# Letting each store wait for its own tile's product alone, in a streaming SwiGLU kernel

## Chip, cores and metric

The kernel runs on one core of a Trainium2 chip. The metric is device time in microseconds (us). The profile's span runs from the first to the last instruction of one profiled execution and is 1.8 us shorter than the time of that same execution. A ratio is the mean time of one kernel's fast runs over that of the other's fast runs of the same rounds, so it is not quite the ratio of the medians that are quoted beside it.

## The reference

```python
def setup_inputs():
    return {"x": np.random.randn(8192, 8192).astype(np.float32)}

def reference(x):
    a, b = np.split(x, 2, axis=-1)
    silu_b = b / (1 + np.exp(-b))
    return a * silu_b
```

It reads 268 MB, writes 134 MB, and does one activation and one product for each output element.

## The kernel before

The rows are cut into 32 tiles of 128 partitions with two rows each. Three slots in SBUF, the on-chip memory, take turns. Every load and store is split over the core's 16 DMA engines, each of which moves its share piece by piece (one partition's bytes are one piece, 64 KB for a whole load). SyncE's transfers go through the queue q1, ScalarE's through q10. SyncE issues the loads; ScalarE applies silu in place and issues the stores of tiles 0 to 29; VectorE multiplies. One semaphore, `prod`, counts all products, and a store waits until it has reached the count known at the moment when the store is written down:

```python
    def store(i, eng, c0=0, cw=R * half):
        s = i % BUFS
        eng.wait_ge(prod_sem, counts["prod"])
        inst = eng.dma_start(
            out=ov[i * P : (i + 1) * P, c0 : c0 + cw], in_=slots[s][:, c0 : c0 + cw]
        )
        # ... (completion to store_sem, or to end_sem for the last three tiles)

        # ... (the first three loads)
        for i in range(last):                    # last = 31
            # ... (tile 0 is computed in two halves)
                swiglu(i)
            if i == last - 1:
                swiglu(last, 0, 1)               # first half of tile 31
            store(i, nc.scalar if i < last - 1 else nc.sync)
            # ... (load of tile i + 3; tile 31 comes in two halves)
        store(last, nc.sync, 0, half)            # called 31a below
        for c0 in range(0, half, half // 2):
            swiglu(last, 1, 2, c0, half // 2)    # third and fourth quarter of tile 31
        store(last, nc.sync, half, half)         # called 31b below
        nc.sync.wait_ge(end_sem, 16 * counts["end"])
```

The first half of tile 31 is written down between tile 30's product and its store. So store 30 waits for 33 products, though 32 would do. Every other store already waits for its own tile alone.

Of the kernel before, what the change touches and what calls it, by code (L numbers as in the profile page):

```python
# [1 line left out]

# [4 lines left out]

_SILU = mybir.ActivationFunctionType.Silu


@with_exitstack
def kernel(
    ctx: ExitStack,
    tc: tile.TileContext,
    x: bass.AP,
    out: bass.AP,
):




    nc = tc.nc
    N, M = x.shape
    half = M // 2
    P = nc.NUM_PARTITIONS
    R = 2
    BUFS = 3

    xv = x.tensor.reshape([N // R, R * M]).ap()  # L30
    ov = out.tensor.reshape([N // R, R * half]).ap()
    ntiles = N // (P * R)
    last = ntiles - 1

    pool = ctx.enter_context(tc.tile_pool(name="sbuf", bufs=1))
    slots = [pool.tile([P, R * M], x.dtype, name=f"slot{s}") for s in range(BUFS)]
    load_sem = [tc.alloc_semaphore(f"load{s}") for s in range(BUFS)]
    store_sem = [tc.alloc_semaphore(f"store{s}") for s in range(BUFS)]
    last_sem = tc.alloc_semaphore("last")
    gate_sem = tc.alloc_semaphore("gate")  # L40
    prod_sem = tc.alloc_semaphore("prod")
    end_sem = tc.alloc_semaphore("end")

    def load(i, c0=0, cw=R * M):
        s = i % BUFS
        if i >= BUFS:
            nc.sync.wait_ge(store_sem[s], 16 * (i // BUFS))
        nc.sync.dma_start(  # L48
            out=slots[s][:, c0 : c0 + cw], in_=xv[i * P : (i + 1) * P, c0 : c0 + cw]
        ).then_inc(last_sem if c0 else load_sem[s], 16)  # L50

    counts = {"gate": 0, "prod": 0, "end": 0}

    def rows(ap, k0, k1, pitch, c0, cw):
        return ap[:, k0 * pitch : k1 * pitch].rearrange("p (r w) -> p r w", w=pitch)[
            :, :, c0 : c0 + cw
        ]

    def swiglu(i, k0=0, k1=R, c0=0, cw=half):
        s = i % BUFS  # L60
        xt = slots[s]
        b = rows(xt, k0, k1, M, half + c0, cw)
        if i == last and k0:
            nc.scalar.wait_ge(last_sem, 16)
        else:
            nc.scalar.wait_ge(load_sem[s], 16 * (i // BUFS + 1))
        nc.scalar.activation(out=b, in_=b, func=_SILU).then_inc(gate_sem, 1)  # L67
        counts["gate"] += 1
        if k0:
            nc.vector.wait_ge(prod_sem, counts["prod"])  # L70
        nc.vector.wait_ge(gate_sem, counts["gate"])  # L71
        nc.vector.tensor_mul(  # L72
            out=rows(xt, k0, k1, half, c0, cw), in0=rows(xt, k0, k1, M, c0, cw), in1=b
        ).then_inc(prod_sem, 1)
        counts["prod"] += 1

    def store(i, eng, c0=0, cw=R * half):
        s = i % BUFS
        eng.wait_ge(prod_sem, counts["prod"])
        inst = eng.dma_start(  # L80
            out=ov[i * P : (i + 1) * P, c0 : c0 + cw], in_=slots[s][:, c0 : c0 + cw]
        )
        if i + BUFS <= last:
            inst.then_inc(store_sem[s], 16)
        else:
            inst.then_inc(end_sem, 16)
            counts["end"] += 1

    with tc.tile_critical(no_gpsimd_drain=True):  # L89
        for i in range(BUFS):  # L90
            load(i)
        for i in range(last):
            if i == 0:
                for k in range(R):
                    swiglu(i, k, k + 1)
            else:
                swiglu(i)
            if i == last - 1:
                swiglu(last, 0, 1)
            store(i, nc.scalar if i < last - 1 else nc.sync)  # L100
            nxt = i + BUFS
            if nxt < last:
                load(nxt)
            elif nxt == last:
                load(last, 0, M)
                load(last, M, M)
        store(last, nc.sync, 0, half)
        for c0 in range(0, half, half // 2):
            swiglu(last, 1, 2, c0, half // 2)
        store(last, nc.sync, half, half)  # L110
        nc.sync.wait_ge(end_sem, 16 * counts["end"])


# [1 line left out]
_INS = ['x']  # L115
_OUTS = [((8192, 4096), 'float32')]


# [23 lines left out]
```

## Time and profile before

| what | value |
|---|---|
| time, median of the first 3 runs | 936.82 us (936.62 to 937.01) |
| span of the profiled run | 935.0 us |
| moved | 402.67 MB |
| DMA engines | busy in every slice, 434 to 435 GB/s in the middle |
| VectorE, ScalarE busy | 30%, 24% |

Such a page is read from the resource that is never idle. Here it is the 16 DMA engines. The shares of VectorE and ScalarE only say that they are not it. The lines stand in the prediction below. Three more of this profile: SyncE's own waits (total us, times, longest), the page's row of the single 4 MB store of SyncE (the last number is the us from issue to landing), and a window of 1.5 us around the moment in question (columns as in the prediction):

```profile
SPq L80 <- DVE slot L72: 37.0, 2, 29.6
...
out_dram<-slot SPq DMA_DIRECT2D x1, 4096.0 KB, 11.3
...
912.50:914.00 1.50, 0.29 (x1) 0.00 (x0) 0.00 (x0) 1.00 0.83 350
```

The longest wait, 29.6 us, is the one ahead of store 30. In the trace's transfer records, cut into half microseconds, the 1.5 us around its end (912.5 to 914.0) are the only place between 50 us and the very end where the 16 engines together are busy for less than 97%.

### The profile page before, as it was taken

What the parts mean: (1) busy time and instruction counts of PE and PEld (TensorE: products, weight loads), DVE (VectorE), ACT (ScalarE), POOL (GpSimd) and SP (SyncE); (2) the same over time, 40 slices, a digit from 0 to 9 for tenths busy, and PEclk for the clock granted to TensorE, in tenths of its full rate; (3) what the DMA queues carried; (4) which work ended last, traced back from release to release, by engine and by line L of the source; (5) the groups of instructions that cost most, each with busy time, mean ns of one, the idle gap of its engine ahead of it and who ended that gap; (6) DMA issues with size and microseconds to landing.
All of it is one profiled execution on the core that took longest, in us unless ns stands there. A gap on an engine that the chain in (4) does not pass through costs nothing.

```text
span 935.0 us, 192 instructions
## 1 busy us (share of the span) xinstructions
DVE 278.6 (30%) x35; ACT 226.6 (24%) x36; POOL 0.2 (0%) x4
## 2 busy tenths in 40 slices
DVE  0333213332133321333312333123331233321352
ACT  0233320233302333113331133311333203332041
POOL 0000000000000000000000000000000000000000
DMA  9999999999999999999999999999999999999998
GB/s 404 401 446 428 429 440 428 436 428 450 426 423 444 428 439 436 430 429 457 422 423 451 414 446 430 429 437 435 428 437 450 414 453 419 432 443 426 428 443 366
DMA packets 9505, 402.67 MB, mean 431 GB/s; under 512 B 1056, under 2 KB 1056, under 8 KB 1056
## 3 DMA queue, kind: packets, MB, share of 16 engines
q1 hardware_dynamic: 5184, 276.83, 68.6%
q10 hardware_dynamic: 4320, 125.83, 31.2%
q14 instruction: 1, 0.01, 0.0%
HBM read 268.44 MB, written 134.22 MB: 431 GB/s over the span
## 4 chain that ended last, share of the span: by engine, by line
DMA 81%; DVE 10%; ACT 8%; issue 0%; SPq 0%; DVEq 0%
DMA slot<-in_x_dram 41%; DMA out_dram<-slot 39%; DVE slot L72 10%; ACT slot L67 8%; SPq L48 0%; SPq L137 0%; DVEq L71 0%; SPq L89 0%
## 5 line engine op out<-in xcount | busy, mean ns | idle before, releaser
L72 DVE TENSOR_TENSOR slot<-slot 128x8192 f32<-128x8192 f32 (+2 forms) x35 | 278.6, 7961 | 642.4 <-ACT slot L67 642.3
L67 ACT ACTIVATE slot<-slot 128x8192 f32<-128x8192 f32 (+2 forms) x35 | 225.3, 6443 | 690.6 <-DMA slot<-in_x_dram 690.6
L67 ACT ACT_TABLE_LOAD x1 | 1.3, 1283 | 0.9 <-SPq L89 0.9
L126 POOL MEMSET const-bfloat16-1.0<- 128x1 bf16 x1 | 0.1, 101 | 0.0
L126 POOL MEMSET const-uint8-127<- 128x1 uint8 x1 | 0.1, 101 | 0.0
L126 POOL MEMSET const-float32-0.0<- 128x1 f32 x1 | 0.1, 98 | 0.2 <-issue 0.2
L126 POOL MEMSET const-float32-1.0<- 128x1 f32 x1 | 0.1, 98 | 0.0
## 6 DMA issues: line engine op xcount, KB each, us to landing
out_dram<-slot ACTq DMA_DIRECT2D x30, 4096.0 KB, 36.7
slot<-in_x_dram SPq DMA_DIRECT2D x2, 4096.0 KB, 27.0
out_dram<-slot SPq DMA_DIRECT2D x1, 4096.0 KB, 11.3
out_dram<-slot SPq DMA_DIRECT2D x2, 2048.0 KB, 14.2
slot<-in_x_dram SPq DMA_DIRECT2D x31, 34.4
```

The costliest lines, as they stand in the source:

```text
L67: nc.scalar.activation(out=b, in_=b, func=_SILU).then_inc(gate_sem, 1)
L72: nc.vector.tensor_mul(out=rows(xt, k0, k1, half, c0, cw), in0=rows(xt, k0, k1, M, c0, cw), in1=b).then_inc(prod_sem, 1)
L126: nc = _bacc.Bacc("TRN2", target_bir_lowering=False, num_devices=1)
```

## The change

Each store is to wait for its own tile's product count. Only the wait of store 30 becomes another: 32 in place of 33.

```diff
     counts = {"gate": 0, "prod": 0, "end": 0}
+    done = {}
@@ swiglu
         counts["prod"] += 1
+        done[i] = counts["prod"]
@@ store
-        eng.wait_ge(prod_sem, counts["prod"])
+        eng.wait_ge(prod_sem, done[i])
```

## The prediction

> **What bounds the kernel now.** I read the page first, then a table of windows over the steady part, then the timeline of the last 40 us, then windows well under a microsecond wide around the two moments that matter. From the page:
>
> ```profile
> span 935.0 us, 192 instructions
> DVE 278.6 (30%) x35; ACT 226.6 (24%) x36; POOL 0.2 (0%) x4
> DMA  9999999999999999999999999999999999999998
> q1 hardware_dynamic: 5184, 276.83, 68.6%
> q10 hardware_dynamic: 4320, 125.83, 31.2%
> ```
>
> VectorE and ScalarE work for less than a third of the span; the 16 DMA engines are busy in every slice. q1 is the queue of SyncE (all loads, and the last three stores), q10 that of ScalarE (30 stores). The windows (columns: stretch, width, busy time of DVE, ACT, POOL, clock, share of the DMA engines, GB/s) say how full:
>
> ```profile
> 100.00:500.00 400.00, 121.70 (x14) 98.41 (x14) 0.00 (x0) 1.00 1.00 435
> 500.00:880.00 380.00, 113.00 (x13) 91.38 (x13) 0.00 (x0) 1.00 1.00 434
> ```
>
> Share 1.00: there is no gap to close in the middle. The compute time that the chain of waits shows lies beside other tiles' transfers. Only the head, the tail, or a gap near the tail can give anything, and nothing but the tail is touched. The timeline of the tail (start, length, engine, line, operation):
>
> ```profile
> 894.85 8.69 DVE L72 TENSOR_TENSOR slot<-slot 128x8192 f32<-128x8192 f32 x1 [20.31 <-ACT slot L67]
> 904.71 3.62 ACT L67 ACTIVATE slot<-slot 128x4096 f32<-128x4096 f32 x1 [9.90 <-DMA slot<-in_x_dram]
> 908.36 4.42 DVE L72 TENSOR_TENSOR slot<-slot 128x4096 f32<-128x4096 f32 x1 [4.82 <-ACT slot L67]
> 912.81 8.59 SPq L80 DMA_DIRECT2D out_dram<-slot  x3
> 914.42 3.71 ACT L67 ACTIVATE slot<-slot 128x2048 f32<-128x2048 f32 x2 [6.09 <-DMA slot<-in_x_dram]
> 916.43 4.62 DVE L72 TENSOR_TENSOR slot<-slot 128x2048 f32<-128x2048 f32 x2 [3.65 <-ACT slot L67]
> ```
>
> Tile 30's product ends at 894.85 + 8.69 = 903.54, but its store is issued at 912.81, after the product of tile 31's first half (908.36 + 4.42 = 912.78). So the needless wait is real, 9.25 us long. But is any DMA engine short of work meanwhile? Until about 912.4 none is: load 31 still runs. Around 913 some are:
>
> ```profile
> 912.45:912.78 0.33, 0.33 (x1) 0.00 (x0) 0.00 (x0) 1.00 0.01 0
> 912.78:912.84 0.06, 0.01 (x1) 0.00 (x0) 0.00 (x0) 1.00 2.54 1092
> 912.84:913.65 0.81, 0.00 (x0) 0.00 (x0) 0.00 (x0) 1.00 0.00 0
> 913.65:913.81 0.16, 0.00 (x0) 0.00 (x0) 0.00 (x0) 1.00 6.75 2867
> 913.81:913.98 0.17, 0.00 (x0) 0.00 (x0) 0.00 (x0) 1.00 0.00 0
> 913.98:914.06 0.08, 0.00 (x0) 0.00 (x0) 0.00 (x0) 1.00 1.91 819
> ...
> 932.59:932.80 0.21, 0.00 (x0) 0.00 (x0) 0.00 (x0) 1.00 2.57 1092
> 932.80:932.86 0.06, 0.00 (x0) 0.00 (x0) 0.00 (x0) 1.00 1.28 546
> ```
>
> In such a table a transfer counts where it starts, so GB/s times width, over the piece size (32 KB for these loads and store 30, 16 KB for the half stores of tile 31), counts the pieces begun. 912.78:912.84: 1092 x 0.06 = 65.5 KB, two pieces. Nothing for 0.81 us. 913.65:913.81: 2867 x 0.16 = 459 KB, fourteen pieces. 913.98:914.06: 819 x 0.08 = 65.5 KB, two again. At the end, fourteen last pieces of 16 KB (229 KB) start by 932.80 and two last ones after it.
>
> So the engines are not alike. Fourteen finish load 31 early, stand idle, and begin store 30 at 913.65 to 913.81. **Two engines are late**: they start their last load piece at 912.78 to 912.84. A piece takes 1.213 us (the DMA view of 904 to 912.45: 99.6% of 16 engines' 8.45 us over 111 data pieces), so they end it at 914.00 to 914.05 and go straight on at 913.98 to 914.06. They have no gap. Followed from piece to piece in the transfer records (each next one starts within 0.01 us of the last one's end), they are also the two that start last at the end, and so end last.
>
> **What the Trainium skill says.** "DMA: Bandwidth & Descriptors", section "Queues, rings and completion order": SP and ACT each own one row of rings, one ring on each of the same 16 engines, and on each engine descriptors are consumed in ring order. That decides where an early store 30 goes: behind load 31, which is in the same rings. The trace agrees: the halves of load 31, issued at 882.3 and 882.7 on q1, were seen complete by ScalarE at 904.71 and 914.42, 9.7 us apart, which is 4.19 MB at 432 GB/s: one after the other. The same page, "Latency and other measured facts", gives about 0.6 us from issue to first byte for this kind of queue; here it is 912.81 to 913.65, 0.84 us. Its "Where 436 GB/s comes from" gives 435.2 GB/s as the ceiling; the windows show 434 and 435. "Perfetto Trace Analysis", section "DMA Instruction — HWDGE (DVE, Sync)", says that the reported instruction covers the issue alone and that the data moves outside it; here an issue takes 0.33 to 0.43 us while store 30 lands 11.3 us later.
>
> **The change, part by part.** For tiles 0 to 29 and both halves of tile 31 the remembered count equals the latest one at the store, so the same wait is built; the instruction listings of the two kernels agree in order and number on every engine. One constant changes: store 30 waits for 32 products instead of 33. Removed: 912.81 - 903.56 = 9.25 us of waiting on SyncE ahead of store 30. Nothing is added. SyncE then issues store 30 at 903.57 and waits for the next product as before, so store 31a still goes at about 912.8 to 913.2 and store 31b at 921.07.
> Step 1, the load: store 30 stands behind load 31 in the ring, so load 31 still lands at 914.4. Cost 0.
> Step 2, the fourteen: they go from their last load piece straight to store 30. From the trace's transfer records, sorted by time, their last load pieces end from 912.44 to 913.47, so they gain 0.2 to 1.2 us each. In half-microsecond bins from 912.0 the records show 0.99, 0.60, 0.22 and 0.63 of the engines busy, so 0.5 x (0.01 + 0.40 + 0.78 + 0.37) = 0.78 us averaged over all 16.
> Step 3, the two: no gap, gain 0. From 914.00 each still has eight pieces of store 30 and two times eight half-size pieces of tile 31: 8 x 1.215 + 16 x 0.614 = 19.5 us (piece times from the records), to 933.5; the records end at 933.46. Unchanged.
> Step 4, does tile 31's second half become the end? The earliest engine then ends store 30 at 912.44 + 8 x 1.215 = 922.2 and store 31a at 922.2 + 8 x 0.614 = 927.1. Store 31b is issued at 921.07 and can start by 921.9. It is in time on every engine: cost 0.
> Sum: a store waits for all 16 engines, and the last two do not move: 0 us, perhaps -0.1. I predict **936.75 us**, against 936.82.
>
> **The rivals.** (a) **The gap is a gap**: the engines' mean gap of 0.78 us, or the largest of 1.2, comes off the time: 936.0 or 935.6. For it: nearly all engines are idle there, and the late two might be late only by chance in one execution. Against: two gapless engines end last in this trace, and pieces are tied to engines, so the early ones cannot take over.
> (b) **Interleaving**: an early store 30 shares with load 31b instead of queueing. Load 31b would then land up to 9.1 us later, 923.5; 6.65 us of compute (914.40 to 921.05) and 0.84 us of issue bring 31b's store to 931.0, and its 4.9 us of movement to 935.9 instead of 933.46: +2.4 us, 939.2. Against: the two halves of load 31 went strictly in turn.
> (c) **Mixed traffic**: early stores beside the late loads slow the late two. Against: the middle of the run mixes both all the time at 434 and 435 GB/s. Worth 0.1 us at most.
>
> **Range and chances.** The three runs of before spread over 0.39 us, and the after runs may sit elsewhere by as much. No change 75%, (a) in part or whole 20%, (b) or (c) 5%. The range is **935.9 to 937.3**: it holds (a)'s mean gap but not (b). Two per cent is 18.7 us, twice the whole wait removed; faster 0.005, within 2% 0.99, slower 0.005.
>
> **What would show it.** Right: the issue group of SyncE starts at about 903.57 instead of 912.81 and still ends at about 921.4; SyncE's waits on products become three, the longest about 20.4 us instead of 29.6; store 30's issue to landing grows from 11.3 to about 20.5 us while it lands at the same 924.1; ScalarE still starts tile 31's second half at 914.4; pieces start throughout 912.84 to 913.65; at the end fourteen engines finish up to 1.2 us ahead of two late ones; the span stays 935.0. Wrong: a span of 934.2 or less (then late engines are no bound, (a)), or ScalarE's last activations after 915 (then (b)).

## The result, and the profile after

| | before | after |
|---|---|---|
| median of 6 runs | 936.75 us (936.39 to 937.55) | 936.76 us (936.48 to 937.75) |
| ratio | | 1.0001 (0.9988 to 1.0014) |
| span of the profiled run | 935.0 us | 935.5 us |

The time is the same. The page of the kernel after:

```profile
span 935.5 us, 192 instructions
DVE 278.6 (30%) x35; ACT 226.6 (24%) x36; POOL 0.2 (0%) x4
DMA  9999999999999999999999999999999999999998
```

The timeline of its last 40 us (start, length, engine, line, operation) answers to the one in the prediction:

```profile
895.36 8.69 DVE L73 TENSOR_TENSOR slot<-slot 128x8192 f32<-128x8192 f32 x1 [20.29 <-ACT slot L68]
904.08 17.83 SPq L82 DMA_DIRECT2D out_dram<-slot  x3
905.22 3.62 ACT L68 ACTIVATE slot<-slot 128x4096 f32<-128x4096 f32 x1 [9.90 <-DMA slot<-in_x_dram]
908.87 4.43 DVE L73 TENSOR_TENSOR slot<-slot 128x4096 f32<-128x4096 f32 x1 [4.82 <-ACT slot L68]
914.91 3.71 ACT L68 ACTIVATE slot<-slot 128x2048 f32<-128x2048 f32 x2 [6.08 <-DMA slot<-in_x_dram]
```

Store 30 is now issued at 904.08, right after its own product (895.36 + 8.69 = 904.05), and no longer after the product that ends at 908.87 + 4.43 = 913.30. So 9.2 us of waiting are gone. (By the clock of the span the issue moved by 8.7 us alone, as the whole tail of this execution lies 0.5 us later.) Everything else keeps its distance: ScalarE's two activations of tile 31 start 9.69 us apart (9.71 before). SyncE's waits, the row of the 4 MB store, and the same window, of the kernel after:

```profile
SPq L82 <- DVE slot L73: 37.9, 3, 21.1
...
out_dram<-slot SPq DMA_DIRECT2D x1, 4096.0 KB, 20.5
...
912.50:914.00 1.50, 0.80 (x1) 0.00 (x0) 0.00 (x0) 1.00 1.17 502
```

The one long wait has become two, and the sum of all three (the wait of store 31b is in it, before and after) has hardly moved: 37.0 to 37.9 us. Counted from its product the store is issued 9.2 us earlier, and it takes 9.2 us longer to land: it stands in the queue. The window has filled. (A transfer counts in it where it starts, so a narrow window can show over 1.00.) The gap is closed, and the end has not moved.

Where did the gap's 0.78 us go? The trace records every piece that a DMA engine moves, with start and duration but without the engine's name. Each engine's share of a transfer ends with a 4-byte write that counts up the semaphore, so the 16 such writes of the last store give the end of each engine's last piece of the whole run. This table is worked out from those records and from the starts of ScalarE's activations; it is not a view of the profile:

```
                                     before   after   after again (e1)
first engine's last piece ends       933.22   932.11   931.87
mean of the 16                       933.32   932.48   932.34
last engine's last piece ends        933.46   933.86   933.10
ScalarE starts the third quarter     914.42   914.91   914.05
last end minus that start             19.04    18.95    19.05
mean end minus that start             18.90    17.57    18.29
```

Before the change all engines finish within 0.24 us of each other. After it they finish spread over 1.75 us: the mean engine ends 0.6 to 1.3 us earlier, counted from the landing of the last load, and the last engine by less than 0.1 us. The end follows the landing of load 31, as ScalarE saw it, by 19.0 us in all three profiles, and that landing is itself set by the latest engine: its last load piece ended at 914.05, 914.45 and 913.69 in the three, and ScalarE started 0.36 to 0.46 us later. The gap was real, but it was slack of the engines that were ahead.

### The profile page after: what moved, and what is told of

It is laid out like the page before. It is cut to its first block, busy times and chain, and to the rows that moved or that the text cites. A ratio compares the mean times of both kernels' runs of the same rounds, so it can differ in the third digit from the quotient of the medians.

```text
span 935.5 us, 192 instructions
## 1 busy us (share of the span) xinstructions
DVE 278.6 (30%) x35; ACT 226.6 (24%) x36; POOL 0.2 (0%) x4
## 2 busy tenths in 40 slices
DMA packets 9505, 402.67 MB, mean 430 GB/s; under 512 B 1056, under 2 KB 1056, under 8 KB 1056
## 4 chain that ended last, share of the span: by engine, by line
DMA 81%; DVE 10%; ACT 8%; issue 0%; SPq 0%; DVEq 0%
DMA slot<-in_x_dram 42%; DMA out_dram<-slot 39%; DVE slot L73 10%; ACT slot L68 8%; SPq L48 0%; SPq L139 0%; DVEq L72 0%; SPq L91 0%
## 6 DMA issues: line engine op xcount, KB each, us to landing
out_dram<-slot SPq DMA_DIRECT2D x1, 4096.0 KB, 20.5
```

## The experiments

My theory (T): the run ends when the latest DMA engine has done its own pieces; that engine had no gap before, so closing the others' gap gives nothing. The rivals are named in the expectations. Each edit is shown against the changed kernel.

**e1, the changed kernel once more.** No edit.

> The changed kernel once more, to narrow the interval. My theory (the latest DMA engines have no gap before the change, so the idle time of the others is slack): 0.0 us against before, within 0.3. Rival A (the engines' mean gap of 0.78 us comes off the time, hidden so far by the scatter): -0.8 us, ratio 0.9992. In the profile both expect no idle stretch of the DMA engines around the end of the last load; mine expects the engines' last pieces to end spread over more than 1 us.

Measured: 936.66 us (936.02 to 936.85, 5 runs) against 936.81 us (9 runs), ratio 0.9998 (0.9984 to 1.0012). That interval alone does not exclude rival A's 0.9992. All executions of the two kernels that I have (24 before, counting those beside e1 and beside e5 to e7, and 11 after) have means of 936.75 and 936.77 us and standard deviations of 0.39 and 0.45. The difference is 0.01 us with a standard error of the square root of 0.39²/24 + 0.45²/11, 0.16 us. A gain of 0.78 us would be five standard errors away. The transfer records show no idle stretch, and last pieces ending over 1.2 us, as T has it. From its timeline, the issue of store 30 and the start of the third quarter:

```profile
903.22 17.82 SPq L82 DMA_DIRECT2D out_dram<-slot  x3
...
914.05 3.71 ACT L68 ACTIVATE slot<-slot 128x2048 f32<-128x2048 f32 x2 [6.11 <-DMA slot<-in_x_dram]
```

**e2, e3, e4: the wait made longer, in three doses.**

```diff
 # e2
         eng.wait_ge(prod_sem, done[i])
+        if i == last - 1:
+            eng.wait_ge(gate_sem, counts["gate"] + 1)
 # e3
-        eng.wait_ge(prod_sem, done[i])
+        eng.wait_ge(prod_sem, done[i] + 2 * (i == last - 1))
 # e4
-        eng.wait_ge(prod_sem, done[i])
+        eng.wait_ge(prod_sem, done[i] + 3 * (i == last - 1))
```

> Store 30 waits longer than in the kernel before: for the activation of the third quarter of tile 31, some 916.3 instead of 912.8 us. All 16 engines should now stand idle before store 30. My theory: the first piece starts 0.84 us after the issue and 19.6 us of stores follow on every engine, so the span grows by 916.3 + 20.6 - 933.46 = 3.4 us, to about 940.2 us; that is slope 1 above the issue time of before and slope 0 below it. Rival B (the order of issue near the end does not matter because the stores of tile 31 end last anyway, at 921.07 + 12.4): 0.

> The same with a later product: store 30 waits for that of the third quarter of tile 31, 918.75 us. My theory: 918.75 + 20.6 - 933.46 = +5.9 us, to about 942.7 us. Rival B: 0, as store 31b's own issue at 921.07 does not move.

> Store 30 waits for the last product of all, 921.07 us, so all three last stores are issued together. My theory: 921.07 + 20.6 - 933.46 = +8.2 us, to about 945.0 us; the late engines' lead in work is gone and all 16 wait. Rival B: about 0 to 1, for the issue of the last store moves by two issue times alone.

Measured: 940.24 us (ratio 1.0036, 1.0023 to 1.0049), 942.70 us (1.0064, 1.0051 to 1.0077) and 945.06 us (1.0089, 1.0075 to 1.0103), beside 936.81 us for before. By the medians that is +3.4, +5.9 and +8.3 us, where T had said +3.4, +5.9 and +8.2. Rival B, that the last store ends last anyway, is out. The issue of store 30 in the timelines of e2, e3 and e4:

```profile
916.76 4.99 SPq L84 DMA_DIRECT2D out_dram<-slot  x3
...
918.42 2.66 SPq L82 DMA_DIRECT2D out_dram<-slot  x3
...
921.07 1.79 SPq L82 DMA_DIRECT2D out_dram<-slot  x3
```

The last piece of the run ends at 937.33, 939.00 and 941.64: 20.57 us after the issue each time. And here all 16 engines end within 0.16 us: all of them had stood idle, and began store 30 within 0.16 us of each other. So the end is the later of two times:

- landing of load 31 (seen by ScalarE) + 19.0 us, where the issue is early (before, after, e1);
- issue of store 30 + 20.57 us, where it is late (e2 to e4).

For the kernel before these are 914.42 + 19.0 = 933.42 and 912.81 + 20.57 = 933.38. It stood just at the kink, the point where one time takes over from the other: a wait longer by 3.6 us (in e2 the issue comes 11.70 us after ScalarE starts on tile 31, in before 8.10 us) cost 3.4 us, and one shorter by 9.2 us gave nothing.

**e5, store 30 as early, but on ScalarE's queue.**

```diff
+            store(i, nc.scalar)
             if i == last - 1:
                 swiglu(last, 0, 1)
-            store(i, nc.scalar if i < last - 1 else nc.sync)
```

> Store 30 as early as in the changed kernel (about 903.6 us), but issued by ScalarE on its queue q10, not behind load 31 in q1. My theory (the early store is harmless only because it stands behind load 31 in the same rings): store 30 and load 31b alternate piece by piece, the late engines end their eighth load piece 15 pieces of 1.213 us after 904.3, at 922.5, so ScalarE starts the last quarters at about 922.8 instead of 914.4, the last store is issued at 929.5 and the end comes at 935.3 instead of 933.46: +1.9 us, about 938.7 us. Rival C (the DMA engines are full either way, so the queue doesn't matter): 0.

Measured: 937.65 us (936.92 to 938.55, 5 runs) against 936.74 us, ratio 1.0009 (0.9996 to 1.0023). It was run on another chip. The direction is T's, and the size is half of what I said; by this interval rival C is not excluded. (Against all 24 executions of before the mean is 0.83 us higher, with a standard error of 0.30: probably longer, but not sure.) What the queue does to the load is seen in the timeline, and in a window just before the end:

```profile
903.73 0.34 ACTq L82 DMA_DIRECT2D out_dram<-slot  x1
904.88 3.62 ACT L68 ACTIVATE slot<-slot 128x4096 f32<-128x4096 f32 x1 [9.90 <-DMA slot<-in_x_dram]
...
912.98 15.84 SPq L82 DMA_DIRECT2D out_dram<-slot  x2
921.82 3.71 ACT L68 ACTIVATE slot<-slot 128x2048 f32<-128x2048 f32 x2 [13.33 <-DMA slot<-in_x_dram]
...
925.00:929.00 4.00, 3.42 (x2) 0.53 (x1) 0.00 (x0) 1.00 0.59 250
```

The two activations are now 16.94 us apart and no longer 9.7 us: load 31's second half was made to share, and landed 7.2 us late. 16.94 us is 14 pieces of 1.213 us. I had counted 15 on the latest engine and added its lag, which made it 922.8; the last store was issued at 928.48 and the end came at 934.39, 5.9 us later. The records add two things. Store 30's first piece started at 907.20, 3.5 us after the issue. And the load's last piece ended at 920.25, but its last completion was written at 921.45 only, one store piece later: the completion too took its turn. So the early store does nothing to the load where it stands behind it in the same queue, and delays it by 7.2 us beside it; how much of this reaches the time is not settled. That the DMA engines are full either way is not the whole story: in e5 they ran dry while tile 31's last product was awaited (share 0.59 in the window from 925 to 929 us).

**e6, every store one tile late.** What store 30 did before, done for all tiles.

```diff
-        eng.wait_ge(prod_sem, done[i])
+        eng.wait_ge(prod_sem, counts["prod"])
@@
+        for k in range(R):
+            swiglu(0, k, k + 1)
         for i in range(last):
-            if i == 0: ...  else: swiglu(i)
-            if i == last - 1:
+            if i + 1 < last:
+                swiglu(i + 1)
+            else:
                 swiglu(last, 0, 1)
             store(i, nc.scalar if i < last - 1 else nc.sync)
```

(A first form of it would have deadlocked: ScalarE issued the store ahead of the activation that the store was to wait for.)

> Every store waits for the next tile's product, as only store 30 did in the kernel before. A slot then cycles through load, own compute, the wait for the next product, and store. Two chains of tiles take turns: over two tiles' time, 2 x 29.1 us, one chain has 15.7 us of compute and some 4 us of latency and so 38 us for its load and store, which need 29.1 us at the full rate; so the DMA engines can just be kept full. My theory (a needless wait costs only where a late engine runs dry): within 1%, 937 to 946 us. Rival D (a wait of a tile's time at each store adds to the slot's cycle of 87 us): 87 to 116 us, +33%, about 1240 us.

Measured: 1038.27 us (1037.31 to 1040.72, 4 runs), ratio 1.1089 (1.1073 to 1.1104). My "within 1%" was wrong, and rival D's +33% too. A window of the middle, and a stretch of the chain of waits in order of time:

```profile
500.00:900.00 400.00, 111.37 (x13) 84.35 (x12) 0.00 (x0) 1.00 0.94 388
...
433.57 8.70 DVE slot L73
442.27 0.02 issue
442.29 22.64 DMA out_dram<-slot
464.93 0.02 issue
464.95 26.33 DMA slot<-in_x_dram
491.28 0.02 issue
491.31 7.04 ACT slot L68
```

Two chains of tiles take turns with a cycle of 7.04 + 8.70 + 22.64 + 26.33 = 64.7 us for two tiles, 32.4 us a tile. The DMA engines are idle for 6% of the time, so my balance of 38 us against 29.1 us did not hold; and when they are busy they move 388 / 0.94 = 413 GB/s and not 435. The records show the second part as well: after the first 20 us, 893 of the 64 KB load pieces took over 2.7 us (2.418 is usual, and the kernel before has 18 such), together 44 us for each engine. They come in bunches, just after a store's issue and again some 22 us later, when the next load begins. Why a piece is slow there I have not settled. The same needless wait costs over 3 us a tile where buffers have to come back in time, and nothing where the last tile alone has it.

**e7, ScalarE's queue used before the first store.**

```diff
+        nc.scalar.dma_start(
+            out=slots[2][:, 0:512], in_=xv[2 * P : 3 * P, 0:512]
+        ).then_inc(warm_sem, 16)
         for i in range(BUFS):
-            load(i)
+            # ... (load 2 without these columns; silu of tile 2 waits for warm_sem too)
```

> The changed kernel with 2 KB of each row of tile 2 loaded by ScalarE at the start, so that q10 has been used long before the first store. In both traces every DMA engine takes 3.3 to 4.2 us instead of 2.4 for one piece just when q10 is first used (about 39 to 41 us), some 1.2 us lost on each. Theory E (first use of the queue's rings is what costs): about -1.1 us, 935.7 us. Rival F (any start of a store stream beside the loads costs that, or the piece only waits for its place): 0.

Measured: 936.94 us (935.94 to 937.19, 5 runs), ratio 1.0001 (0.9988 to 1.0013). The interval's lower end just touches theory E's -1.1 us; against all 24 executions of before the mean differs by 0.01 us, with a standard error of 0.23, so theory E is out as to the time. The records say the same: 16 slow pieces remain, at 37.0 to 37.5 us, 1.0 us lost on each engine, where the other profiles of the changed kernel have 19. So this is no better kernel. Its profiled run, with a span of 934.2 us, is a fourth case for the law above: the last piece ends at 932.56, 19.03 us after ScalarE starts the third quarter at 913.53.

No version beat the two kernels. With 402.67 MB at 435 GB/s, 925.7 us of the span of 935.0 us are movement, and some 9 us are left in all.

## Why the prediction was right

The prediction was 936.75 us with a range of 935.9 to 937.3; measured were 936.76 us. That the two agree to 0.01 us is luck, as single executions scatter by 0.4 us; that nothing was gained is not. By its steps:

- *What bounds it* held: the middle is full before and after (share 1.00), and only the window around 913 us changed.
- *One constant changes, 9.25 us of waiting go*: 9.2 us went.
- *Step 1*, the store stands behind load 31 in the ring: the load's halves were seen 9.69 us apart (9.71 before) and the store took 20.5 us to land, as said. e5 shows what happens otherwise.
- *Step 2*, the early engines gain 0.2 to 1.2 us each, 0.78 us in the mean: the mean end came 1.33 us (after) and 0.61 us (e1) earlier, counted from the landing of the last load. The size was of the one execution that was read; it changes with the lags.
- *Step 3*, the late engines gain nothing: the last end stayed 19.0 us behind that landing in four profiles (before, after, e1, e7). The number two was of that one execution: in the profile after, thirteen engines end by 932.52, two at 933.1, and one at 933.86.
- *Step 4*, store 31b is in time: the records of after and e1 show no idle stretch on any engine before its last piece.

Its signs came about half a microsecond late, as the whole tail of this profile did: a span of 935.5 us for 935.0, a landing of store 30 at 924.6 for 924.1, and ScalarE at 914.91, close below the 915 that would have spoken for rival (b). The two activations are 9.69 us apart, so it was not (b).

I had given rival A 20%, since the late engines could have been late by chance. A sum over the profiles of before, after and e1 says why the last engine should not be a matter of chance here. The needless wait of store 30 began with that same engine: tile 31's first half had to land, and the latest engine decides when. From there to the first possible piece of store 30 it is 8.10 us (904.71 to 912.81) and 0.84 us more; from the same landing to the next the second half takes 9.71 us. In the records this engine's last load piece ends at 914.05, and store 30 could start at 913.65: the latest engine was still loading. In the profile after the same sum gives 905.22 + 8.10 + 0.84 = 914.16 against a last load piece that ended at 914.45; in e1, whose activations start at 904.32 and 914.05, 913.26 against 913.69. So it would have had no gap there either. This sum for after and e1 is argued from their numbers, as the old wait did not run in those executions.

The scatter between executions stays open in part. The profile after ended 0.5 us later than that of before. In its records one engine's completion of the loads lags the first engine's by 2.38 us at 827 us and by 3.05 us at 885 us, and between them, at 851.0 us, lies the one 8 KB transfer of the instruction queue (q14, 0.31 us). In the profile of before this transfer came at 849.8, and the last engine's lag did not change (2.31 and 2.30 us). It fits that the transfer fell on the latest engine once and not the other time, but the lag grew by 0.67 us, more than the transfer's 0.31 us, and no run tested it.

## What to carry to other kernels

A wait that lasts 9 us is worth nothing by that alone: ask which engine would have worked in that time, and whether it is the one that ends last. Where 16 DMA engines share a transfer, a gap in their mean can be slack of the early ones; look at the last one, and try the wait longer as well as shorter, for a kink tells where the path turns. Here an early store left the load that mattered alone when it stood behind it in the same queue, and delayed it when it ran beside it in the other.

## What the Trainium skill lacked or had wrong

- No page says that the 16 engines keep their lags for a whole run, though the end of a kernel is set by the latest. In the records of after, the last engine's completion of one load came 2.36 to 2.39 us behind the first's for every load that landed between 102 and 827 us. For the halves of tile 31, with one queue at work, it was 1.2 to 1.8 us (before, after and e1), and after the change the engines ended the run about as far apart (1.75 and 1.24 us).
- "DMA: Bandwidth & Descriptors", "Issuing engines are not separate DMA queues", says that DMAs issued by several engines interleave, with which e5 agrees, and that issuing from several engines only saves issue time. The second is too narrow: in e5 the same store at the same time on the other queue delayed the load by 7.2 us, since it went beside the load and not behind it.
- The same page, "Latency and other measured facts", has about 0.6 us to the first byte. From the start of the issue to the first piece it was 0.84 to 0.85 us in before, e2, e3 and e4, where store 30 met idle engines; the page does not say from where it counts.
- No page that I read says that 64 KB pieces slow down when a stream begins or ends on the other queue beside them: e6 lost 44 us on each engine in 893 pieces over 2.7 us (2.418 is usual), begun 0.9 to 3.4 us after an issue in the cycle that I looked at. The cause is open.
